# Seven products in place of eight in five of eleven weight blocks of the down projections

## Chip, cores and metric

The kernel runs on one core of a Trainium2 chip. The metric is device time in microseconds (us), the median over runs. One execution was also recorded by the hardware profiler; its durations are used to explain the time.

## What is computed

A trunk of two layers over 256 tokens of width 1024, all in float32. Each layer is a SwiGLU feed-forward (FFN), a mixer (a convolution module in the first layer, latent attention in the second) and another FFN, so there are four FFNs. The part that matters here:

```python
D_MODEL, SEQ, D_FF = 1024, 256, 2816

def swiglu_ffn(h, w1, w3, w2):
    return (jax.nn.silu(h @ w1) * (h @ w3)) @ w2

h = h + 0.5 * swiglu_ffn(rmsnorm(h, g), w1, w3, w2)     # twice in each layer
```

The last product, `@ w2`, is the down projection: (256 x 2816) times (2816 x 1024).

## The kernel before

**Precision.** TensorE is fed with float32r operands. Each float32 operand x is split into `hi`, x rounded to float32r, and `lo = x - hi`. A product of two split operands takes three matmuls into the same accumulator (`mm3`: lo x hi, hi x hi, hi x lo). For weights the split runs on the chip: `load` brings a block of 128 x 2048 float32 (1 MB) into a `raw` buffer by a DMA issued from SyncE (SP), ScalarE casts it to `hi` (two pieces of 1024 columns), and VectorE subtracts to get `lo` (two pieces). There are four `raw` buffers and four pairs of `hi`/`lo` buffers, used in rotation: a raw buffer comes free when its last `lo` is made, a `hi`/`lo` pair when the last matmul that reads it is done.

**One FFN.** In the up part, steps c = 0 to 5 make gate and up columns of the hidden layer. Steps 0 to 4 use four weight blocks each, step 5, half as wide, uses two. For each half of the tokens (tb = 0, 1) the result is multiplied to `g` (VectorE), transposed in 32 x 32 squares (VectorE, `gt`), written to DRAM and read back (`gd`, `gb`, DMAs from SP) and split into `Gh` (ScalarE) and `Gl` (VectorE). This is `turn`. In the down part (`Rows`), eleven weight blocks of `w2` follow, each with two k tiles (128 rows of `w2`) and all 1024 output columns. Four PSUM banks `o[tb, d]` accumulate, one for each half of the tokens and half of the columns. A block is 2 k tiles x 2 token halves x 2 column halves = 8 products of 3 matmuls, 24 matmuls of 512 columns. `block` does blocks 0 to 8; `finish` does blocks 9 and 10 accumulator by accumulator, adds each to the residual `h`, and lets the next stage begin (squares for its norm, transposes `tp` of `h` on TensorE).

**What sets the order.** A scheduler in the build puts the instructions of each engine into one fixed queue. An engine carries out its queue strictly in that order, so an instruction that waits holds up all behind it on the same engine. SP's queue is the order in which DMAs are issued. `urgent` pieces are pulled ahead, and `behind` holds the weight splits back behind them.

Of the kernel before, what the change touches and what calls it, by code (L numbers as in the profile page):

```python
# [41 lines left out]
PIECES = 2  # L42

BEHIND = 6


CONV_DVE = ((0, 0, 31), (2, 0, 31), (4, 0, 31), (5, 0, 31), (7, 0, 13))
# [31 lines left out]
def trunk(ctx: ExitStack, tc: tile.TileContext, x, xt, pos, invf, gains, gfin, wdw,  # L79
# [28 lines left out]
    for i in range(2):  # L108
        for w13, w2 in ((f1w13, f1w2), (f2w13, f2w2)):

            for cc_ in range(5):
                for m in range(2):
                    blocks += [w13[i, m, 2 * cc_ + a_] for a_ in range(2)]
            blocks += [w13[i, a_, 10] for a_ in range(2)]
            blocks += [w2[i, a_] for a_ in range(NF // 2)]
# [24 lines left out]
            order(ins, first)  # L140

    def load(src, pieces=1):
        if isinstance(src, tuple):
            raw = rawp.tile([P, HB], F32, tag="raw", name=uid("raw"))
            nc.sync.dma_start(raw, src[1])
            return raw
        n = src.shape[-1]
        raw = rawp.tile([P, HB], F32, tag="raw", name=uid("raw"))
        hi = wp.tile([P, HB], F32R, tag="hi", name=uid("hi"))
        lo = wp.tile([P, HB], F32R, tag="lo", name=uid("lo"))  # L150
        if len(loaded) < 7:
            fetch(raw[:, :n], src)
        else:
            nc.sync.dma_start(raw[:, :n], src)
        for i in range(pieces):
            c = slice(i * n // pieces, (i + 1) * n // pieces)
            behind(nc.scalar.copy(hi[:, c], raw[:, c]))  # L157
            behind(nc.vector.tensor_sub(lo[:, c], raw[:, c], hi[:, c].bitcast(F32)))  # L158
        return hi, lo

    def urgent(f):

        def g(*args, **kw):
            traced = nc.cur_bb.bb.instructions
            n = len(traced)
            with tc.high_priority():
                r = f(*args, **kw)
            last = {ins.engine: ins for ins in traced[n:]}
            for engine, ins in last.items():
                ahead_of.setdefault(engine, []).append(ins)  # L170
            return r
        return g

    def load_ahead(ahead=W_BUFS - 2):
        load_to(min(len(blocks), n_used[0] + ahead))
# [5 lines left out]
    def weights(n=1, more=True):  # L181
        out = []
        for _ in range(n):
            n_used[0] += 1
            if more:
                load_ahead()
# [279 lines left out]


    class Rows:
        def __init__(self, zh, zl, nk, last=False):
            self.zh, self.zl, self.nk, self.last = zh, zl, nk, last  # L470
            self.o = {(tb, d): bank("A", "o") for tb in range(NT) for d in range(2)}

        def mm(self, part, i, tb, d, o, f0, f1, o0=0, o1=512, after=()):
            hi, lo = part
            for j in range(2):
                f = 2 * i + j
                c = slice(j * D + d * 512 + o0, j * D + d * 512 + o1)
                mm3(o, self.zh[:, f, tbs(tb)], self.zl[:, f, tbs(tb)], hi[:, c], lo[:, c], f == f0, f == f1 - 1,
                    after)

        def block(self, i):
            part, = weights()
            for tb in range(NT):
                for d in range(2):
                    apart = self.last and (tb, d) == (1, 1)
                    self.mm(part, i, tb, d, self.o[tb, d], 0, self.nk - (4 if apart else 0))

        def finish(self, rh, make_next, act):
            nb = self.nk // 2
            parts = weights(2)  # L490

            def add(tb, c, o):
                if rh is None:
                    nc.vector.tensor_add(h[tb][:, c], o, h[tb][:, c])
                else:
                    nc.vector.scalar_tensor_tensor(h[tb][:, c], o, rh[tb], h[tb][:, c],
                                                   op0=ALU.mult, op1=ALU.add)

            if self.last:

# [3 lines left out]
            for i, (tb, d) in enumerate((tb, d) for tb in range(NT) for d in range(2)):  # L504
                halves = self.last and i == 3
                for o0, o1 in ((0, 256), (256, 512)) if halves else ((0, 512),):
                    o, f0 = (bank("B", "o")[:, :256], self.nk - 4) if halves else (self.o[tb, d], 0)
                    for a, part in enumerate(parts):
                        after = nxt.turned if i == 3 and a == 1 and not self.last else ()
                        self.mm(part, nb - 2 + a, tb, d, o, f0, self.nk, o0, o1, after)  # L510
# [15 lines left out]
    def ffn_in(act, X, make_next, beside):  # L526
        Gh = act.tile([P, NF, S], F32R, tag="Gh", name=uid("Gh"))
        Gl = act.tile([P, NF, S], F32R, tag="Gl", name=uid("Gl"))
        def turn(c, tb, w, g):


# [6 lines left out]
                nc.sync.dma_start(dv[i], t[32 * i:32 * i + 32, :w].rearrange("p (j c) -> p j c", j=4))  # L538
            b = act.tile([P, 512], F32, tag="gb", name=uid("gb"), bufs=3)
            nc.sync.dma_start(b[:, :w], d)  # L540
            f = slice(4 * c, 4 * c + n)
            bv = b[:, :w].rearrange("p (i t q) -> p t i q", i=4, q=32)
            gh = Gh[:, f, tbs(tb)].rearrange("p t (i q) -> p t i q", q=32)
            nc.scalar.copy(gh, bv)  # L544
            nc.vector.tensor_sub(Gl[:, f, tbs(tb)].rearrange("p t (i q) -> p t i q", q=32), bv, gh.bitcast(F32))  # L545

        for c in range(6):

# [45 lines left out]
        o = Rows(Gh, Gl, NF, make_next is Final)  # L594
        for i in range(NF // 2 - 2):
            o.block(i)
            beside()
        return o.finish(X.rh, make_next, act)


    def conv(X, make_next):
# [300 lines left out]
    def mla_in(act, X, make_next, cc, sn):  # L902
# [162 lines left out]
        for i in range(2, H + 3):  # L1065
# [5 lines left out]
                values(i - 3, pt[i - 3])  # L1071
            if i in (6, 8):
                o.block((i - 6) // 2)
        return o.finish(None, make_next, act)


    dw = const.tile([P, KT, TAPS], F32, name="dw")
# [121 lines left out]
```

## Time and profile before

| what | value |
|---|---|
| median of 3 runs | 939.93 us (939.67 to 942.21) |
| span of the profiled execution, first to last instruction | 937.9 us |
| granted TensorE clock, mean | 0.997 of full speed |
| TensorE (PE) busy | 925.9 us, 99% of the span |
| VectorE (DVE) busy | 578.2 us, 62% |
| ScalarE (ACT) busy | 493.8 us, 53% |
| GpSimd (POOL) busy | 85.0 us, 9% |
| HBM read and written | 203 GB/s over the span |

The profiled execution's own device time isn't listed apart from its span. The span is 2.0 us below the median of the runs and 1.8 below the fastest; these 2.0 us lie outside the first and last instruction. Matmuls are pipelined: a matmul's listed duration contains time in which the next one already runs, so that a busy share of 99% says that TensorE never waits long, and the pace is read from the starts.

### The profile page before, as it was taken

To read this page: it belongs to the slowest core of one execution; us is meant where nothing else is said; L and a number is where in the kernel's file an instruction comes from. 1 tells how busy PE (TensorE), PEld (TensorE's weight loads), DVE (VectorE), ACT (ScalarE), POOL (GpSimd) and SP (SyncE) were. 2 spreads that over 40 slices of the span, in tenths; PEclk is the share of its full clock that TensorE was granted. 3 is DMA by queue.
4 is the path that set the end of the run, shared out by engine and by line. 5 is a ranking of instruction groups with operands and counts; after the bars stand their busy time and mean duration, and the time that the engine had idled before them with its cause. 6 is when DMAs were issued, how large, how long until landed. Compare 5 with 4: busy or idle time off the path is not lost.

```text
span 937.9 us, 12057 instructions
## 1 busy us (share of the span) xinstructions
PE 925.9 (99%) x4397; PEld 771.7 (82%) x4397; DVE 578.2 (62%) x911; ACT 493.8 (53%) x844; POOL 85.0 (9%) x209
## 2 busy tenths in 40 slices
PE   9999999999999999999999999999999999999997
PEld 6888888898967888888888888888898788888885
DVE  5776664489975655664466666545666576656643
ACT  6964453468865445443374454444666475445431
POOL 1000000059920000000000000000200000000000
PEclk9999999999999999999999999999999999999998
DMA  9986775524324777775547777753441557767611
GB/s 343 355 284 237 245 251 199 179 91 141 130 90 172 277 230 244 245 247 206 197 149 256 239 251 246 236 201 118 180 180 51 189 204 252 244 230 258 233 45 45
DMA packets 60394, 191.54 MB, mean 204 GB/s; under 512 B 11184, under 2 KB 33328, under 8 KB 40752
## 3 DMA queue, kind: packets, MB, share of 16 engines
q1 hardware_dynamic: 59760, 190.09, 58.1%
q8 instruction: 34, 0.56, 0.2%
q10 hardware_dynamic: 576, 0.69, 0.2%
q14 instruction: 24, 0.20, 0.1%
HBM read 178.17 MB, written 12.58 MB: 203 GB/s over the span
## 4 chain that ended last, share of the span: by engine, by line
PE 93%; ACT 3%; DMA 1%; issue 1%; DVE 1%; POOL 1%; SPq 0%; POOLq 0%; ACTq 0%
PE u L240 17%; PE u L244 17%; PE u L243 17%; PE o L240 10%; PE o L243 9%; PE o L244 9%; PE gate L621 3%; PE u L621 3%; PE o L805 2%; ACT hi L157 1%; PE tp L281 1%; DMA raw<-in_f1w 1%; PE a L244 1%; PE a L240 1%; PE a L243 1%
## 5 line engine op out<-in xcount | busy, mean ns | idle before, releaser
L158 DVE TENSOR_TENSOR lo<-raw,hi 128x1024 fp32r<-128x1024 f32 (+1 forms) x290 | 338.9, 1211 | 203.1 <-ACT hi L157 203.0
L157 ACT CAST hi<-raw 128x1024 fp32r<-128x1024 f32 (+1 forms) x290 | 288.1, 1047 | 270.5 <-PE u L244 140.2
L240 PE MATMUL u<-lo,Xh 128*128 128x512 f32 x688 | 268.1, 390 | 0.0
L244 PE MATMUL u<-hi,Xl 128*128 128x512 f32 x688 | 267.7, 390 | 0.4 <-DVE Xl L299 0.4
L243 PE MATMUL u<-hi,Xh 128*128 128x512 f32 x688 | 267.7, 389 | 0.0
L244 PEld LDWEIGHTS u<-hi,Xl 128*128 128x128 f32 x688 | 129.1, 188 | 27.7 <-DVE Xl L299 0.9
L240 PEld LDWEIGHTS u<-lo,Xh 128*128 128x128 f32 x688 | 129.2, 188 | 27.3 <-DVE lo L158 0.5
L243 PEld LDWEIGHTS u<-hi,Xh 128*128 128x128 f32 x688 | 129.2, 188 | 26.5
L243 PE MATMUL o<-hi,Gh 128*128 128x512 f32 (+1 forms) x356 | 137.8, 387 | 0.0
L244 PE MATMUL o<-hi,Gl 128*128 128x512 f32 (+1 forms) x356 | 137.7, 387 | 0.0
L240 PE MATMUL o<-lo,Gh 128*128 128x512 f32 (+1 forms) x356 | 137.3, 387 | 0.0
L244 PEld LDWEIGHTS o<-hi,Gl 128*128 128x128 f32 x356 | 66.9, 188 | 13.6
L243 PEld LDWEIGHTS o<-hi,Gh 128*128 128x128 f32 x356 | 66.9, 188 | 13.4
L240 PEld LDWEIGHTS o<-lo,Gh 128*128 128x128 f32 x356 | 66.8, 188 | 13.4
L272 POOL TENSOR_TENSOR ms<-ss 128x1 f32<-128x1 f32 x16 | 4.6, 287 | 644.5 <-ACT junk L267 644.5
L545 DVE TENSOR_TENSOR Gl<-gb,Gh 128x512 fp32r<-128x512 f32 (+1 forms) x48 | 30.8, 644 | 39.2 <-ACT Gh L544 39.2
L544 ACT CAST Gh<-gb 128x512 fp32r<-128x512 f32 (+1 forms) x48 | 27.9, 584 | 50.8 <-DMA gb<-gd 50.8
L665 DVE SCALAR_TENSOR_TENSOR acc<-V,dw,acc 128x256 f32<-128x256 f32 (+1 forms) x160 | 53.9, 417 | 0.0
L683 ACT ACTIVATE prod<-V,dw 128x128 f32<-128x128 f32 (+1 forms) x121 | 46.1, 421 | 2.9 <-POOL odd L684 1.3
L592 DVE TENSOR_TENSOR g<-s,u 128x512 f32<-128x512 f32 (+1 forms) x48 | 30.7, 639 | 15.9 <-PE u L244 15.5
L590 ACT ACTIVATE s<-u,R 128x512 f32<-128x512 f32 (+1 forms) x48 | 31.2, 650 | 5.9 <-ACT Gh L544 3.0
L534 DVE STREAM_TRANSPOSE gt<-g 128x512 f32<-128x512 f32 (+1 forms) x48 | 32.0, 667 | 1.5
(206 smaller groups left out, 836.1 us busy)
## 6 DMA issues: line engine op xcount, KB each, us to landing
raw<-in_f2w SPq DMA_DIRECT2D x66, 1024.0 KB, 4.9
raw<-in_f1w SPq DMA_DIRECT2D x64, 1024.0 KB, 5.0
raw<-in_cw SPq DMA_DIRECT2D x12, 1024.0 KB, 4.8
gd<-gt SPq DMA_DIRECT2D x160, 64.0 KB, 3.1
gb<-gd SPq DMA_DIRECT2D x40, 256.0 KB, 4.9
raw<-in_wo SPq DMA_DIRECT2D x4, 1024.0 KB, 5.5
raw<-in_wuq SPq DMA_DIRECT2D x3, 1024.0 KB, 4.8
raw<-in_f1w SPq DMA_DIRECT2D x8, 256.0 KB, 6.1
```

Of the source, the lines that this page charges most:

```text
L157: behind(nc.scalar.copy(hi[:, c], raw[:, c]))
L158: behind(nc.vector.tensor_sub(lo[:, c], raw[:, c], hi[:, c].bitcast(F32)))
L240: mm = nc.tensor.matmul(o, ah, bl, start=start, stop=False)
L243: nc.tensor.matmul(o, ah, bh, start=False, stop=False)
L244: return nc.tensor.matmul(o, al, bh, start=False, stop=stop)
L534: nc.vector.transpose(t[:, :w], g[:, :w].rearrange("p (t j q) -> p j t q", t=n, q=32))
L545: nc.vector.tensor_sub(Gl[:, f, tbs(tb)].rearrange("p t (i q) -> p t i q", q=32), bv, gh.bitcast(F32))
L590: nc.scalar.activation(s[:, :w], u[0, tb][:, :w], AF.Silu, scale=X.r[tb])
L592: nc.vector.tensor_mul(g[:, :w], s[:, :w], u[0, tb][:, w:] if both else u[1, tb])
L621: mm = nc.tensor.matmul(u[:, t], w[:, c], X.x[:, k, t], start=(k == 0), stop=(k == KT - 1))
L665: nc.vector.scalar_tensor_tensor(out if j == j1 - 1 else y, v, w, y, op0=ALU.mult, op1=ALU.add)
L683: nc.scalar.activation(p, v, AF.Copy, scale=w)
```

## The change

In blocks 0, 2, 4, 6 and 8 of each down part (the list `FAST`) the eight products become seven by Strassen's scheme in Winograd's form. The 2 x 2 structure is: token halves, the two k tiles of the block, and column halves. It needs sums of the quarters of the weight block (each 128 x 512) and sums of the hidden activations' tiles (128 x 128).

- Weights: a fast block takes two raw buffers and two `hi`/`lo` pairs. Of the raw block three quarters are split (`raw` pair); four sums of quarters are made and split (`sums` pair). GpSimd makes two of the sums in one add of 1024 columns, VectorE the other two in two adds of 512.
- Activations: in the up part, after tb = 1 of steps 0 to 4, GpSimd makes four differences of 128 x 128 (`combine`), which are split by ScalarE and VectorE (`Sh`, `Sl`, and the place in `Gh`, `Gl` of a tile that is no longer needed itself).
- Four of the seven products accumulate over the fast blocks in PSUM banks of their own (`p`: three banks of tag B, one of tag C). After block 8, `fold` adds them to `h` in the right combinations (one copy on ScalarE, four operations on VectorE, four on GpSimd).
- The factor 0.5 / rms, until now applied at the end in `finish`, is applied to `g` in `turn`'s caller.
- `load_ahead` counts slots, so that a fast block counts for two; the SBUF reserve for descriptors of dynamic DMAs is set to 1024.

The core of the diff:

```diff
+FAST = (0, 2, 4, 6, 8)
...
+    def load_fast(src):
+        raw = rawp.tile([P, HB], F32, tag="raw", name=uid("raw"))
+        sums = rawp.tile([P, HB], F32, tag="raw", name=uid("sums"))
+        nc.sync.dma_start(raw, src)
+        v = raw.rearrange("p (b n) -> p b n", n=512)
+        t = sums.rearrange("p (b n) -> p b n", n=512)
+        behind(nc.gpsimd.tensor_tensor(t[:, 0:2, :], v[:, 0:4:3, :], v[:, 1:2, :].to_broadcast([P, 2, 512]), op=ALU.add))
+        behind(nc.vector.tensor_add(t[:, 2, :], t[:, 0, :], v[:, 3, :]))
+        behind(nc.vector.tensor_add(t[:, 3, :], t[:, 2, :], v[:, 2, :]))
+        out = []
+        for x, cols in ((raw, ((0, 512), (1024, 2048))), (sums, ((0, 1024), (1024, 2048)))):
+            hi = wp.tile([P, HB], F32R, tag="hi", name=uid("hi"))
+            lo = wp.tile([P, HB], F32R, tag="lo", name=uid("lo"))
+            for c0, c1 in cols:
+                behind(nc.scalar.copy(hi[:, c0:c1], x[:, c0:c1]))
+                behind(nc.vector.tensor_sub(lo[:, c0:c1], x[:, c0:c1], hi[:, c0:c1].bitcast(F32)))
+            out.append((hi, lo))
+        return out
...
         def block(self, i):
-            part, = weights()
+            part, = weights(1, True, W_BUFS - 1)
...
+        def fast(self, i):
+            n = FAST.index(i)
+            (raw, sums), = weights()
+            if n == 0:
+                self.p = [bank(t, "p") for t in "BBBC"]
...
+            for o, key, (ah, al), (hi, lo), q in (
+                    (self.p[0], "p1", z(f, 0), raw, 0), (self.o[0, 0], (0, 0), z(f + 1, 0), raw, 2),
+                    (self.o[0, 1], (0, 1), s(2), raw, 3), (self.p[2], "p5", z(f, 1), sums, 0),
+                    (self.p[3], "q7", s(1), sums, 1), (self.p[1], "q6", s(0), sums, 2),
+                    (self.o[1, 0], (1, 0), z(f + 1, 1), sums, 3)):
+                c = slice(q * 512, q * 512 + 512)
+                mm3(o, ah, al, hi[:, c], lo[:, c], self.begin(key), isinstance(key, str) and i == FAST[-1])
+            if i == FAST[-1]:
+                self.fold()
...
+        def combine(i, b0, b1):
...
+            sub(v[:, 3], b1[:, 0], b1[:, 1])
+            sub(v[:, 0], b0[:, 0], v[:, 3])
+            sub(v[:, 1], b1[:, 0], b0[:, 0])
+            sub(v[:, 2], b0[:, 1], v[:, 0])
+            split(Sh[:, 3 * n:3 * n + 3, :], Sl[:, 3 * n:3 * n + 3, :], sx[:, :3, :])
+            split(Gh[:, 2 * i, tbs(1)], Gl[:, 2 * i, tbs(1)], sx[:, 3, :])
...
-                nc.vector.tensor_mul(g[:, :w], s[:, :w], u[0, tb][:, w:] if both else u[1, tb])
+                nc.vector.scalar_tensor_tensor(g[:, :w], u[0, tb][:, w:] if both else u[1, tb], X.rh[tb], s[:, :w],
+                                               op0=ALU.mult, op1=ALU.mult)
...
-    nc = _bacc.Bacc("TRN2", target_bir_lowering=False, num_devices=1)
+    nc = _bacc.Bacc("TRN2", target_bir_lowering=False, num_devices=1, dynamic_dma_scratch_size=1024)
```

How the queues change is shown at three places, all in the second FFN (the one behind the convolution; the others read alike). The numbers in the names tell tiles apart. Before, `raw_3650`, `raw_3682`, `raw_3714`, `raw_3746`, `raw_3778` and `raw_3810` are blocks 0 to 5. After, `raw_3697`, `raw_3832`, `raw_3903` and `raw_3974` with `sums_3698`, `sums_3833`, `sums_3904` and `sums_3975` are the fast blocks 0, 2, 4 and 6; `raw_3850` and `raw_3921` are the plain blocks 3 and 5.

**VectorE at the start of the down part.** Before, from `g` of step 5 on:

```order
L592 TENSOR_TENSOR g_3618<-s_3616,u_3566 128x256
L534 STREAM_TRANSPOSE gt_3620<-g_3618 128x256
L545 TENSOR_TENSOR Gl_2714<-gb_3546,Gh_2713 128x4x128
L592 TENSOR_TENSOR g_3633<-s_3631,u_3567 128x256
L534 STREAM_TRANSPOSE gt_3635<-g_3633 128x256
L158 TENSOR_TENSOR lo_3684<-raw_3682,hi_3683 128x1024 x2
L545 TENSOR_TENSOR Gl_2714<-gb_3627,Gh_2713 128x2x128
L158 TENSOR_TENSOR lo_3716<-raw_3714,hi_3715 128x1024 x2
```

After, from the same `g` on:

```order
L687 SCALAR_TENSOR_TENSOR g_3767<-u_3715,rh_2767,s_3765 128x256
L624 STREAM_TRANSPOSE gt_3769<-g_3767 128x256
L604 TENSOR_TENSOR Gl_2814<-gb_3684,Gh_2813 128x3x128
L604 TENSOR_TENSOR Gl_2814<-sx_3686,Gh_2813 128x128
L687 SCALAR_TENSOR_TENSOR g_3782<-u_3716,rh_2848,s_3780 128x256
L181 TENSOR_TENSOR lo_3839<-raw_3832,hi_3838 128x512
L624 STREAM_TRANSPOSE gt_3784<-g_3782 128x256
L181 TENSOR_TENSOR lo_3839<-raw_3832,hi_3838 128x1024
L604 TENSOR_TENSOR Sl_2816<-sx_3686,Sh_2815 128x384
L181 TENSOR_TENSOR lo_3845<-sums_3833,hi_3844 128x1024 x2
L162 TENSOR_TENSOR lo_3852<-raw_3850,hi_3851 128x1024
L173 TENSOR_TENSOR sums_3904<-sums_3904,raw_3903 128x512
```

The subtractions for block 2 stand behind the split of step 4's second token half (`gb_3684`) and behind the difference that GpSimd makes of it (`sx_3686`), as before the split for block 1 stood behind `gb_3546`. The add for block 4 stands between the two halves of block 3's split.

**VectorE in the middle of the down part.** Before, blocks 3 to 5 and on:

```order
L158 TENSOR_TENSOR lo_3748<-raw_3746,hi_3747 128x1024 x2
L158 TENSOR_TENSOR lo_3780<-raw_3778,hi_3779 128x1024 x2
L158 TENSOR_TENSOR lo_3812<-raw_3810,hi_3811 128x1024 x2
L158 TENSOR_TENSOR lo_3844<-raw_3842,hi_3843 128x1024 x2
L158 TENSOR_TENSOR lo_3876<-raw_3874,hi_3875 128x1024 x2
```

After, from block 4 to block 6:

```order
L181 TENSOR_TENSOR lo_3910<-raw_3903,hi_3909 128x512
L181 TENSOR_TENSOR lo_3910<-raw_3903,hi_3909 128x1024
L181 TENSOR_TENSOR lo_3916<-sums_3904,hi_3915 128x1024 x2
L162 TENSOR_TENSOR lo_3923<-raw_3921,hi_3922 128x1024
L173 TENSOR_TENSOR sums_3975<-sums_3975,raw_3974 128x512
L162 TENSOR_TENSOR lo_3923<-raw_3921,hi_3922 128x1024
L174 TENSOR_TENSOR sums_3975<-sums_3975,raw_3974 128x512
L181 TENSOR_TENSOR lo_3981<-raw_3974,hi_3980 128x512
```

The first add for block 6 (`L173`), which needs block 6's data from DRAM and GpSimd's sum of it, stands in front of the second half of block 5's split.

**SP's queue at the start of the down part.** Before:

```order
L538 DMA gd_3541<-gt_3539 32x4x128 x4
L540 DMA gb_3531<-gd_3526 128x512
L154 DMA raw_3746<-in_f2w 128x2048
L540 DMA gb_3546<-gd_3541 128x512
L154 DMA raw_3778<-in_f2w 128x2048
```

After:

```order
L630 DMA gb_3669<-gd_3664 128x512
L628 DMA gd_3679<-gt_3677 32x4x128 x4
L158 DMA raw_3850<-in_f2w 128x2048
L630 DMA gb_3684<-gd_3679 128x512
L169 DMA raw_3903<-in_f2w 128x2048
```

The read-back of step 4's second token half stands behind the DMA of block 3 in both. Block 3's raw buffer is now the one that held block 0's sums.

More of the change, by code (lines that the diff above doesn't have):

```diff
@@ L114, in trunk @@
             blocks += [w13[i, a_, 10] for a_ in range(2)]
-            blocks += [w2[i, a_] for a_ in range(NF // 2)]
+            blocks += [("fast", w2[i, a_]) if a_ in FAST else w2[i, a_] for a_ in range(NF // 2)]
             if w13 is f1w13:
@@ L172, in urgent, with slots @@
         return g
+    def slots(b):
+        return 2 if isinstance(blocks[b], tuple) and blocks[b][0] == "fast" else 1
     def load_ahead(ahead=W_BUFS - 2):
-        load_to(min(len(blocks), n_used[0] + ahead))
+        b = n_used[0]
+        while b < len(blocks) and slots(b) <= ahead:
+            ahead -= slots(b)
+            b += 1
+        load_to(b)
     def load_to(last):
@@ L185, in weights @@
             if more:
-                load_ahead()
+                load_ahead(ahead)
             else:
@@ L468, in trunk, with __init__, begin, mm @@
     class Rows:
-        def __init__(self, zh, zl, nk, last=False):
+        def __init__(self, zh, zl, nk, last=False, sh=None, sl=None):
             self.zh, self.zl, self.nk, self.last = zh, zl, nk, last
+            self.sh, self.sl = sh, sl
             self.o = {(tb, d): bank("A", "o") for tb in range(NT) for d in range(2)}
-        def mm(self, part, i, tb, d, o, f0, f1, o0=0, o1=512, after=()):
+            self.begun = set()
+            self.early = max(i for i in range(nk // 2 - 2) if sh is None or i not in FAST)
+        def begin(self, key):
+            first = key not in self.begun
+            self.begun.add(key)
+            return first
+        def mm(self, part, i, tb, d, o, key, f1, o0=0, o1=512, after=()):
             hi, lo = part
```

70 lines of the change are left out of this document (50 added, 20 removed).

## Prediction

> **What bounds the kernel now.** First the page: busy shares and the chain that ended last.
>
> ```profile
> span 937.9 us, 12057 instructions
> PE 925.9 (99%) x4397; PEld 771.7 (82%) x4397; DVE 578.2 (62%) x911; ACT 493.8 (53%) x844; POOL 85.0 (9%) x209
> PE 93%; ACT 3%; DMA 1%; issue 1%; DVE 1%; POOL 1%; SPq 0%; POOLq 0%; ACTq 0%
> ```
>
> TensorE carries 93% of the chain. Whatever takes a matmul out of an unbroken stream shortens the kernel, as long as the stream stays unbroken. How much one matmul is worth is not its listed duration. The group of down-projection matmuls, then the timeline of TensorE where the second FFN's down part begins:
>
> ```profile
> L240 PE MATMUL o<-lo,Gh 128*128 128x512 f32 (+1 forms) x356 | 137.3, 387 | 0.0
> ```
>
> ```profile
> 411.61 0.39 PE L240 MATMUL o<-lo,Gh 128*128 128x512 f32 x1
> 411.84 0.39 PE L243 MATMUL o<-hi,Gh 128*128 128x512 f32 x1
> ...
> 414.33 0.39 PE L240 MATMUL o<-lo,Gh 128*128 128x512 f32 x1
> ```
>
> The last row is the 12th matmul after the first: 2.72 / 12 = 0.2267 us from start to start. The 387 ns include overlap with the next one. So a block of 24 matmuls lasts 5.44 us, a fast one of 21 lasts 4.76 us.
>
> Next, what the other engines do in the middle of this down part (timeline; the bracket is idle time before):
>
> ```profile
> 433.57 2.01 ACT L157 CAST hi<-raw 128x1024 fp32r<-128x1024 f32 x2 [3.43 <-PE o L244]
> 434.65 2.36 DVE L158 TENSOR_TENSOR lo<-raw,hi 128x1024 fp32r<-128x1024 f32 x2 [3.08 <-ACT hi L157]
> 440.10 2.36 DVE L158 TENSOR_TENSOR lo<-raw,hi 128x1024 fp32r<-128x1024 f32 x2 [3.09 <-ACT hi L157]
> ```
>
> Each block costs VectorE 2.36 of 5.44 us, and the split begins as soon as TensorE releases a buffer pair, three blocks ahead of its use. There is room, and the question is whether the new work fits in it.
>
> **What is removed.** 3 matmuls in each of 5 blocks of 4 FFNs: 60 x 0.2267 = 13.6 us off the stream, 3.4 us for each FFN. (By the listed 387 ns it would be 23.2 us, which is wrong here.) A pair of one fast and one plain block takes TensorE 45 x 0.2267 = 10.20 us, where it took 10.88.
>
> **What is added to a fast block.** The prices, by form:
>
> ```profile
> L158 DVE TENSOR_TENSOR lo<-raw,hi 128x1024 fp32r<-128x1024 f32 x286 | 335.9, 1217 | 203.1 <-ACT hi L157 203.0
> L361 DVE TENSOR_TENSOR lo<-raw,hi 128x512 fp32r<-128x512 f32 x8 | 5.5, 688 | 2.3 <-ACT hi L359 2.2
> L157 ACT CAST hi<-raw 128x1024 fp32r<-128x1024 f32 x286 | 285.4, 1051 | 270.5 <-PE u L244 140.2 <-PE o L244 91.9 <-issue 35.3
> L359 ACT CAST hi<-raw 128x512 fp32r<-128x512 f32 x7 | 4.3, 614 | 3.6 <-DMA raw<-in_f1w 3.6
> L684 POOL TENSOR_TENSOR odd<-odd,prod 128x128 f32<-128x128 f32 x44 | 19.9, 456 | 0.5 <-ACT odd L679 0.5
> L684 POOL TENSOR_TENSOR odd<-odd,prod 128x256 f32<-128x256 f32 x14 | 10.2, 728 | 0.0
> ```
>
> ScalarE: one cast of 512 and three of 1024 columns, 0.61 + 3 x 1.05 = 3.8 us; a pair of blocks 5.9 of 10.2, no bound. VectorE: three subtractions of 1024 (1.18 each in a run, 2.36 / 2), one of 512 and two adds of 512 (0.69 each): 5.6 us; with a plain block 8.0 of 10.2. GpSimd's add of 1024 columns isn't in the trace. The two rows grow by 0.272 us for 128 columns, so an estimate is 0.728 + 6 x 0.272 = 2.36 us. The lower end is VectorE's 1.22 for 1024 columns; the upper end, if the strided and repeated operands cost as much again, is 4.7. I take 2.36, the same engine's own slope.
>
> Separately each engine fits. But VectorE and GpSimd get in each other's way. Timelines of the two in the attention layer, where an add of one column on GpSimd (`ms`) falls beside a subtraction and where it doesn't:
>
> ```profile
> 660.74 3.02 DVE L158 TENSOR_TENSOR lo<-raw,hi 128x640 fp32r<-128x640 f32 x4
> 663.15 0.66 POOL L272 TENSOR_TENSOR ms<-ss 128x1 f32<-128x1 f32 x1 [5.81 <-ACT junk L267]
> 667.01 0.19 POOL L272 TENSOR_TENSOR ms<-ss 128x1 f32<-128x1 f32 x1 [2.01 <-ACT junk L267]
> 669.08 4.62 DVE L158 TENSOR_TENSOR lo<-raw,hi 128x1024 fp32r<-128x1024 f32 x4
> 672.52 1.23 POOL L272 TENSOR_TENSOR ms<-ss 128x1 f32<-128x1 f32 x1 [4.14 <-ACT junk L267]
> ```
>
> Alone the add takes 0.19. Beside a subtraction it takes 0.66 and 1.23 and ends at 663.81 and 673.75, just after VectorE's runs end at 663.76 and 673.70. GpSimd's add waits for the subtraction in progress. That VectorE waits for GpSimd too I take as likely; no row shows it. [...]
>
> Taking turns, a pair of blocks needs 8.0 + 2.4 = 10.4 us of the two engines' time against TensorE's 10.2.
>
> **The chain that decides.** The DMAs and the read-back of `g`:
>
> ```profile
> raw<-in_f2w SPq DMA_DIRECT2D x4, 1024.0 KB, 4.8
> ```
>
> ```profile
> gd<-gt SPq DMA_DIRECT2D x160, 64.0 KB, 3.1
> gb<-gd SPq DMA_DIRECT2D x40, 256.0 KB, 4.9
> ```
>
> Block 6's data needs the raw buffer of block 3, since fast blocks take two of the four. And block 5's second subtraction stands in VectorE's queue behind the first add for block 6. So from "block 3 split" to "block 5 split" there is a chain: DMA 4.8, GpSimd's wait for the subtraction in progress 0 to 1.22 (half, 0.6), its add 2.36, block 5's first half 1.18 (held up by that add), VectorE's add 0.69, the second half 1.18, and some 0.3 of hand-overs (six of 0.05, as 663.81 less 663.76): 11.1 us for each 10.2 of TensorE, 0.9 lost. It is run through for 3 to 5 and 5 to 7.
>
> The first pass, block 1 to block 3, is longer. Time 0 is the end of step 4's products, 48 matmuls before 411.61, or 400.73. Without loss block 3 is due at 10.88 + 4.76 + 5.44 + 4.76 = 25.8. How late the read-back of step 4's second half came before:
>
> ```profile
> 405.81 0.32 SPq L540 DMA_DIRECT2D gb<-gd  x1
> 410.81 0.62 ACT L544 CAST Gh<-gb 128x512 fp32r<-128x512 f32 x1 [1.20 <-DMA gb<-gd]
> ```
>
> It was issued at 5.1 and there at 10.1. Now it is issued behind block 3's DMA, which waits for block 0's sums to be split. VectorE does that behind its `g` (to 1.5) and the wait for GpSimd's add for block 2 (to about 3.0): adds 2 x 0.69, transpose 0.7 and two subtractions 2.4 end at 7.5. The read-back is there at about 13, GpSimd's four differences (4 x 0.456) and the casts end at 16, block 2's raw subtractions (behind them in the queue) at 19.3, GpSimd's add for block 4 at 22.2, then block 2's sums 24.6, block 3's first half 25.8, add and second half 27.7. That is 1.9 late (0 if the read-back isn't held up, 3 if DMAs side by side take 6).
>
> Loss for each FFN: 1.9 + 0.9 + 0.9 = 3.7 us, against 3.4 gained. Four FFNs: +14.8 - 13.6 = +1.2 us. The span becomes 939.1, and with the 2.0 us around it the time is 941.1.
>
> **Edits at nothing.** `g` now multiplies by a third factor, and the last adds have one fewer: the same VectorE form either way. The up part gets 1.8 us of GpSimd (4 x 0.456) and some 0.7 of VectorE (smaller pieces of the same split) in each step of 21.8 us (4 x 5.44), with splits three blocks ahead; if that cover were gone, a step could lose these 2.5. `fold` puts some 3 us on VectorE (4 x 0.75) and four adds of 512 columns, 1.27 each, on GpSimd, before `h` is turned:
>
> ```profile
> 464.13 0.75 DVE L496 SCALAR_TENSOR_TENSOR h<-o,rh,h 128x512 f32<-128x512 f32 x1
> 469.42 0.60 PE L281 MATMUL tp<-ident,h 128*128 128x128 f32 x4
> ```
>
> 4.5 us lie between the add to `h` and its first reader; uncovered it would be up to 3 us for each FFN. The smaller descriptor reserve meets queues that the profile's page lists as made in hardware:
>
> ```profile
> q1 hardware_dynamic: 59760, 190.09, 58.1%
> ```
>
> I price it at nothing; were each DMA slower, the chain above would grow by as much.
>
> **Rivals.** *Slack after all:* GpSimd's add and VectorE's work overlap freely. Then block 5's first half and the wait fall out of the chain: 4.8 + 2.36 + 0.69 + 1.18 + 0.3 = 9.3, under 10.2; block 3 isn't late either, as block 2's sums needn't wait for the add for block 4. Losses of 0.2 for each FFN leave 939.9 - 13.6 + 0.8 = 927.1. For it: GpSimd's waits are the only ones shown. Against it: those two waits. *Slower, GpSimd's add is long:* at its upper end of 4.7 the chain takes 13.4, each pass loses 3.2, the first 1.9 + 2.3: 10.6 for each FFN, 939.9 - 13.6 + 42.4 = 968.7. Each 0.1 over 2.36 costs three passes in four FFNs, 1.2 us, so from 2.5 on the kernel is slower beyond the bound below. For it: nothing in the trace has such operands. Against it: VectorE's price for the same shape is far lower. *Not done:* the products are not fewer, or some matmuls wait for more: 940.
>
> **How the numbers follow.** Changes under 0.3% (2.8 us) are about what a measurement can't tell from none. The forecast, turn-taking with 3.7 lost, has 0.60; its loss lies between 2.0 (half waits, read-back in time) and 5.7 (first pass 3, whole waits), so its own range is 934 to 949, and it splits into faster 0.15, same 0.17, slower 0.28 (with more terms that can grow than shrink). Slack has 0.20 (faster), the long add 0.17 (slower), not done 0.03 (same). Faster 0.35, same 0.20, slower 0.45. The range, 927 to 954, takes in the forecast's own, the first rival's time and the long add up to 3.4 us.
>
> **What would show it.** In the profile after: matmuls still 0.227 apart; idle time of TensorE before blocks 3, 5 and 7 of each down part, put down to `lo`, of 2 and 1 and 1 us; GpSimd's `sums` near 2.4, longer where they meet subtractions; VectorE's subtractions of more than 1.22 beside them; the first add for a fast block waiting for GpSimd. No idle time there would mean slack, and `sums` of over 3 us the long add. Idle time in the up parts or before the transposes would mean that an edit priced at nothing was not.

## The result, and the profile after

The changed kernel took 932.63 us (median of 4, 930.08 to 935.65), the kernel before beside it 939.80: a ratio of 0.9923, interval 0.9896 to 0.995. It is faster; the forecast was 941.1 and leaned to slower. Two of the four times lie at 930 and two at 935. The profiled execution is the one of 930.08 us: 9.6 us of span were gained there of the 13.6 that left the stream, and some 5 fewer in the other two.

The page of after, the lines that answer to those of before:

```profile
span 928.3 us, 12409 instructions
PE 913.5 (98%) x4337; PEld 761.0 (82%) x4337; DVE 687.6 (74%) x1047; ACT 536.4 (58%) x928; POOL 213.4 (23%) x325
PE 89%; DVE 5%; ACT 3%; DMA 1%; issue 1%; SPq 0%; POOLq 0%; ACTq 0%; POOL 0%; DVEq 0%
```

There are 60 matmuls fewer, VectorE's share went from 62% to 74%, GpSimd's from 9% to 23%, and VectorE is now on 5% of the chain where it was on 1%. TensorE's timeline in the second FFN's down part, at the first matmuls of blocks 0, 2 and 7:

```profile
411.13 0.39 PE L271 MATMUL p<-lo,Gh 128*128 128x512 f32 x1
...
421.33 0.39 PE L271 MATMUL p<-lo,Gh 128*128 128x512 f32 x1
...
446.49 0.39 PE L271 MATMUL o<-lo,Gh 128*128 128x512 f32 x1
```

A pair of a fast and a plain block takes 10.20 us, exactly 45 x 0.2267, and blocks 0 to 6 (three pairs and a fast block) 35.36 = 30.60 + 4.76. The stream is unbroken. What TensorE did wait for is in the view of waits (in all, times, longest):

```profile
PE tp L433 <- ACT sigm L422: 2.9, 1, 2.9
PE o L271 <- ACT Oh L1151: 1.3, 2, 0.9
PE o L901 <- ACT Z L837: 1.1, 1, 1.1
```

The first row is new, and no row says `lo` before a down block. So the losses of 1.9, 0.9 and 0.9 us that the prediction put into every FFN aren't there. Where the 4.0 us went, by the times at which TensorE's stages begin:

| stretch | before | after | off the stream | lost |
|---|---|---|---|---|
| to the first down part | 127.06 | 127.24 | 0 | 0.2 |
| first down part, to the transposes of the conv's norm | 58.49 | 58.11 | 3.4 | 3.0 |
| from there to the second down part | 226.06 | 225.78 | 0 | -0.3 |
| to the third down part | 181.41 | 178.52 | 3.4 | 0.5 |
| to the fourth (attention in between) | 277.88 | 275.23 | 3.4 | 0.75 |
| to the end | 67.00 | 63.42 | 3.4 | -0.2 |

Three quarters lie in one place, the end of the first FFN. VectorE's and GpSimd's timelines there:

```profile
169.33 4.60 DVE L162 TENSOR_TENSOR lo<-raw,hi 128x1024 fp32r<-128x1024 f32 x3 [1.59 <-ACT hi L161]
173.85 0.68 DVE L553 TENSOR_TENSOR fold<-p,fold 128x512 f32<-128x512 f32 x1
174.45 1.21 DVE L162 TENSOR_TENSOR lo<-raw,hi 128x1024 fp32r<-128x1024 f32 x1
175.58 0.68 DVE L554 TENSOR_TENSOR fold<-p,fold 128x512 f32<-128x512 f32 x1
176.19 0.67 DVE L556 TENSOR_TENSOR fold<-p,fold 128x512 f32<-128x512 f32 x1
176.78 4.18 DVE L162 TENSOR_TENSOR lo<-raw,hi 128x1024 fp32r<-128x1024 f32 x2
180.88 0.68 DVE L558 TENSOR_TENSOR fold<-p,fold 128x512 f32<-128x512 f32 x1
181.48 1.87 DVE L566 TENSOR_TENSOR h<-o,h 128x512 f32<-128x512 f32 x3
```

```profile
177.60 2.28 POOL L557 TENSOR_TENSOR h<-h,fold 128x512 f32<-128x512 f32 x1
```

VectorE does not pause from 169.33 until the additions to `h` (`L566`) are done. The split of the last down block, `fold`, and the split of two blocks of the next stage stand ahead of them, and one pair of subtractions takes 4.18 in place of 2.36 us because GpSimd's addition of 2.28 lies in it. The second `h` addition starts at 182.1. Before, the same queue held only one split:

```profile
177.31 2.36 DVE L158 TENSOR_TENSOR lo<-raw,hi 128x1024 fp32r<-128x1024 f32 x2 [3.08 <-ACT hi L157]
179.58 0.74 DVE L496 SCALAR_TENSOR_TENSOR h<-o,rh,h 128x512 f32<-128x512 f32 x1
181.66 0.75 DVE L496 SCALAR_TENSOR_TENSOR h<-o,rh,h 128x512 f32<-128x512 f32 x1 [1.33 <-PE o L244]
184.41 0.29 DVE L396 TENSOR_SCALAR dR<-ident,R 128x128 f32<-128x128 f32 x1 [2.00 <-POOL R L275]
```

There the `h` additions waited for TensorE, and the norm's factor (`dR`) was ready at 184.70, 0.85 us before its transposes at 185.55. With 3.4 us off the stream the second addition should have started at about 178.4; it came 3.7 later, less 0.85 of cover: the wait of 2.9. (The row of the wait names `sigm`, a small step that ScalarE does behind the same squares. It ended at 185.24; `dR`, which the transposes read, ended at 185.25.)

### The profile page after: what moved, and what is told of

It is laid out like the page before. It is cut to its first block, busy times and chain, and to the rows that moved or that the text cites. A ratio compares the mean times of both kernels' runs of the same rounds, so it can differ in the third digit from the quotient of the medians.

```text
span 928.3 us, 12409 instructions
## 1 busy us (share of the span) xinstructions
PE 913.5 (98%) x4337; PEld 761.0 (82%) x4337; DVE 687.6 (74%) x1047; ACT 536.4 (58%) x928; POOL 213.4 (23%) x325
## 4 chain that ended last, share of the span: by engine, by line
PE 89%; DVE 5%; ACT 3%; DMA 1%; issue 1%; SPq 0%; POOLq 0%; ACTq 0%; POOL 0%; DVEq 0%
PE u L275 17%; PE u L271 17%; PE u L274 17%; PE o L271 6%; PE o L274 6%; PE o L275 6%; DVE lo L162 3%; PE u L717 3%; PE gate L717 3%; PE p L275 2%; PE p L271 2%; PE p L274 2%; PE o L901 2%; PE y L790 2%; ACT hi L161 1%
## 5 line engine op out<-in xcount | busy, mean ns | idle before, releaser
L162 DVE TENSOR_TENSOR lo<-raw,hi 128x1024 fp32r<-128x1024 f32 (+1 forms) x250 | 304.9, 1255 | 76.9 <-ACT hi L161 76.8
L161 ACT CAST hi<-raw 128x1024 fp32r<-128x1024 f32 (+1 forms) x250 | 248.0, 1046 | 153.3 <-PE u L275 111.1
L271 PE MATMUL o<-lo,Gh 128*128 128x512 f32 (+1 forms) x236 | 91.0, 386 | 0.0
L275 PE MATMUL o<-hi,Gl 128*128 128x512 f32 (+1 forms) x236 | 91.0, 385 | 0.0
L274 PE MATMUL o<-hi,Gh 128*128 128x512 f32 (+1 forms) x236 | 91.0, 385 | 0.0
L172 POOL TENSOR_TENSOR sums<-raw 128x1024 f32<-128x1024 f32 x20 | 53.1, 2653 | 161.2 <-DMA raw<-in_f2w 52.6
L181 DVE TENSOR_TENSOR lo<-sums,hi 128x1024 fp32r<-128x1024 f32 x40 | 56.1, 1433 | 0.0
L180 ACT CAST hi<-sums 128x1024 fp32r<-128x1024 f32 x40 | 40.7, 1052 | 22.5 <-PE u L275 15.3
L604 DVE TENSOR_TENSOR Gl<-gb,Gh 128x512 fp32r<-128x512 f32 (+2 forms) x48 | 33.1, 704 | 26.4 <-ACT Gh L603 26.4
L180 ACT CAST hi<-raw 128x512 fp32r<-128x512 f32 (+1 forms) x40 | 31.4, 834 | 34.7 <-PE o L275 27.8
```

The lines of the kernel that those rows point to most:

```text
L172: behind(nc.gpsimd.tensor_tensor(t[:, 0:2, :], v[:, 0:4:3, :], v[:, 1:2, :].to_broadcast([P, 2, 512]), op=ALU.add))
L180: behind(nc.scalar.copy(hi[:, c0:c1], x[:, c0:c1]))
L181: behind(nc.vector.tensor_sub(lo[:, c0:c1], x[:, c0:c1], hi[:, c0:c1].bitcast(F32)))
L271: mm = nc.tensor.matmul(o, ah, bl, start=start, stop=False)
L274: nc.tensor.matmul(o, ah, bh, start=False, stop=False)
L275: return nc.tensor.matmul(o, al, bh, start=False, stop=stop)
```

## Experiments

Theory A, from that trace: the weights of the down blocks are ready in time, and what is lost lies at the ends of the FFNs, in VectorE's queue. Rival B: VectorE and GpSimd taking turns in the down blocks costs it. Rival C: the prediction's chain.

**The changed kernel again,** twice, for a profile of the longer time and for its spread. Theory D in the second expectation is A with what the first run added; it is spelled out under hold_subs.

> The changed kernel once more, unaltered, beside the others of this call. Its four times stood at two levels, 930.1 and 930.7, and 934.6 and 935.7, and only the lower one has a trace. Theory A (the weights of the down blocks are ready in time; what was not gained, 4.0 of 13.6 us in that trace, lies where an FFN ends: about 3 us where the h additions of the first FFN come behind fold and the next blocks' differences, some 0.5 us each behind the second and third) says nothing of the upper level: a profile at that level should show it in some other place. Rival B (VectorE and GpSimd taking turns in the down blocks): at the upper level TensorE waits for lo or sums in the down blocks, some 5 us in all. Rival C (the prediction's chain, 0.9 us for each pass and 1.9 us for the first): waits of 0.9 us before plain blocks 3, 5 and 7. Expected times: 930 to 936.

> The changed kernel unaltered, beside the next three. Theory D says its time depends on how late the weights of the first FFN run: 930 to 931 where its first down block is fetched by 105 us after the start of the span, 933 to 936 where it is fetched some 2.6 us later.

Measured: 934.50 (933.18 to 936.27, 5 runs) and 931.51 (929.74 to 934.54, 6 runs); ratios 0.9947 (0.9935 to 0.9959) and 0.9915 (0.9903 to 0.9928). With the first four that is a spread from 929.7 to 936.3, not two levels. The profile of `again`, at 934.50: the waits, ScalarE and VectorE where the last down block is split, TensorE at the transposes, and the window from 188 to 190 us (the figure after the five engines is the granted clock):

```profile
PE tp L433 <- ACT sigm L422: 4.8, 1, 4.8
```

```profile
171.22 2.00 ACT L161 CAST hi<-raw 128x1024 fp32r<-128x1024 f32 x2 [5.35 <-DMA raw<-in_f1w]
```

```profile
172.30 2.36 DVE L162 TENSOR_TENSOR lo<-raw,hi 128x1024 fp32r<-128x1024 f32 x2 [2.00 <-ACT hi L161]
```

```profile
188.32 3.45 PE L433 MATMUL tp<-dR,h 128*128 128x128 f32 x16 [4.84 <-ACT sigm L422]
```

```profile
188.00:190.00 2.00, 1.68 (x8) 1.71 (x9) 0.22 (x1) 0.82 (x4) 0.00 (x0) 0.50 0.02 8
```

It is the same place, worse. The last down block's cast came 3 us later (171.22, in after 168.24), now waiting for its data: the DMA was issued 2.6 us later and took 7.1 us to land, in place of 4.9. Why it took longer isn't shown. The whole queue moved, and TensorE waited 4.84 us. Behind this wait its clock is 0.50: the 16 transposes take 3.45 us, in after 2.02. From the conv's second transposes on the two traces run alike. The sum of 4.4 us: 0.98 at the first down part's start, 2.0 more of wait, 1.4 of slow clock. The longer time goes with how late the first FFN's weights run. Four traces of the changed kernel show it (`late`, told below, has one transfer more); the second and third column give when the DMA of block 1 was issued and when that of block 10 had landed:

| trace | block 1 issued | block 10 landed | block 10 split from | wait | clock behind it | time |
|---|---|---|---|---|---|---|
| after | 104.93 | 166.42 | 169.33 | 2.87 | 1.00 | 930.08 |
| again2 | 105.59 | 167.15 | 169.32 | 2.87 | 1.00 | 930.10 |
| late | 106.64 | 169.80 | 170.98 | 4.19 | 0.50 | 934.56 |
| again | 107.52 | 171.12 | 172.30 | 4.84 | 0.50 | 934.50 |

What makes the weights late in one run and not in another is open.

So the expectation of `again` that the upper time has another place was wrong, and rivals B and C, which wanted waits in the down blocks, don't find them in this trace.

**The next stage's blocks held back.** First with casts and differences, at the first FFN's end only:

```diff
-            parts = weights(2)
+            parts = weights(2, n_used[0] > 40)
...
-                        nxt.early(i)
+                        nxt.early(i); i == 0 and load_ahead()
```

> At the end of the first FFN the next two blocks are loaded and split behind the first h addition and not ahead of all of them, so that VectorE goes from fold straight to the h additions. The other FFNs are as they were. Theory A: the wait of 2.9 us ahead of the transposes of the conv's norm goes to under 0.5 us, and the time is 2.4 to 2.9 us below that of the changed kernel (about 927.5 against 930.4, and the same step at the upper level). Rivals B and C: the loss is in the down blocks, and the time stays within 0.5 us.

Measured: 933.99 (932.51 to 934.34), ratio 0.9938 (0.9926 to 0.9949); beside `again` no gain where 2.4 to 2.9 us were expected. The wait was 3.45. ScalarE's timeline tells why:

```profile
179.99 0.63 ACT L298 ACTIVATE junk<-h 128x512 f32<-128x512 f32 x1 [6.04 <-DVE h L566]
180.52 0.19 ACT L298 ACTIVATION_READ_ACCUMULATOR junk<-h 128x1 f32 x1
180.62 3.88 ACT L161 CAST hi<-raw 128x1024 fp32r<-128x1024 f32 x4
184.40 0.63 ACT L298 ACTIVATE junk<-h 128x512 f32<-128x512 f32 x1
```

VectorE's `h` additions now came on time (179.20 and 180.63, each waiting for TensorE), but the held casts went in between the two squares on ScalarE. The wait changed engines, so this run decides nothing. The second form leaves the casts where they were and holds the differences alone:

```diff
...
-            behind(nc.vector.tensor_sub(lo[:, c], raw[:, c], hi[:, c].bitcast(F32)))
+            rest = lambda c=c: behind(nc.vector.tensor_sub(lo[:, c], raw[:, c], hi[:, c].bitcast(F32)))
+            held.append(rest) if holding[0] else rest()
...
+            holding[0] = n_used[0] < 40
             parts = weights(2)
+            holding[0] = False
...
                         nxt.early(i)
+                    while i == 1 and held:
+                        held.pop(0)()
```

> At the end of the first FFN only the differences (lo) of the next two blocks are put behind the second h addition; their casts on ScalarE stay early, so that neither VectorE nor ScalarE has anything of the next stage ahead of the h additions and squares. Theory D: at the upper level the transfers of the first FFN run some 2.6 us late, the last down block is split late, fold, the four differences and the h additions queue up on VectorE, TensorE waits over 3 us for the transposes, and its clock halves for 3 us behind that; at the lower level only the wait of 2.9 us is there. Without the four differences in that queue the wait falls under 1 us and the clock stays: 927.5 to 929.5, against 930.4 and 934.5 of the changed kernel. Rival E: late transfers alone make the upper level, through waits in front of the last down blocks: then these waits stay and the time stays above 932.

Measured: 928.38 (927.61 to 928.64), ratio 0.9879 (0.9862 to 0.9895). The waits have no row for `tp` any more. VectorE's timeline:

```profile
174.02 0.69 DVE L554 TENSOR_TENSOR fold<-p,fold 128x512 f32<-128x512 f32 x1
...
175.95 0.68 DVE L559 TENSOR_TENSOR fold<-p,fold 128x512 f32<-128x512 f32 x1
177.59 0.69 DVE L569 TENSOR_TENSOR h<-o,h 128x512 f32<-128x512 f32 x1 [0.96 <-PE o L276]
179.02 0.69 DVE L569 TENSOR_TENSOR h<-o,h 128x512 f32<-128x512 f32 x1 [0.74 <-PE o L276]
181.79 0.29 DVE L428 TENSOR_SCALAR dR<-ident,R 128x128 f32<-128x128 f32 x1 [2.08 <-POOL R L307]
```

This profile's weights ran late as well: block 10 landed at 170.56, and block 6 began 10.50 us and block 8 10.92 us after the block two before, in place of 10.20. Even so the additions waited for TensorE, nothing was lost at the transposes, and the four times lie within 1.0 us, where the 15 of the changed kernel spread over 6.5. This is the theory's test by removal, and it holds; rival E's 932 is ruled out. The changed kernel was not run beside hold_subs, so that the two are compared by their ratios to the kernel before; beside `late_hold_dve` below it was (`again2`).

The held differences are not free. They now stand ahead of the first part of the next stage's input (`Xp`) in VectorE's queue, and TensorE waits there:

```profile
PE gate L722 <- DVE Xp L445: 0.7, 1, 0.7
```

From the transposes to the second down part this trace takes 226.61 us, 0.8 more than after.

**Four fast blocks in place of five.**

```diff
-FAST = (0, 2, 4, 6, 8)
+FAST = (0, 2, 4, 6)
```

> Blocks 0, 2, 4 and 6 in seven products; block 8 is plain, so that fold comes 10.9 us earlier in each FFN, with four plain blocks behind it. The stream saves 48 matmuls in place of 60, 10.9 in place of 13.6 us. Theory A and D: nothing of fold stands ahead of the h additions any more, the losses at the ends of the FFNs (0.5 to 4.4 us each) are gone, and the time is 939.6 less 10.9, 928.7 to 930: no slower than the changed kernel at its lower level and some 4 us faster than at its upper one. If the loss isn't at the ends of the FFNs, each fast block is worth the same: 2.7 us above the changed kernel, 933 to 937.

Measured: 929.28 (928.75 to 930.17), ratio 0.9891 (0.9876 to 0.9906): 10.3 of the 10.9 us that it takes off the stream, against 7.2 of 13.6 (939.80 less 932.63) of the changed kernel. Its second FFN with what follows it lasts 178.70 us, 181.41 less 12 x 0.2267 to 0.01; in after 0.5 were lost there. Its first FFN had the latest weights of all these traces (block 1 issued at 108.28), and yet no wait for `tp`. Beside the profiled runs of 930, the fifth fast block with `fold` at its end is worth nothing as the change places it.

**The products without the gain.** The product for p5 is issued twice in each fast block.

```diff
+                if key == "p5":
+                    mm3(o, ah, al, hi[:, c], lo[:, c], self.begin(key), False)
```

> The fast blocks issue the product for p5 twice, so that a fast block has 24 matmuls as a plain one has; the preparation, the read-back, GpSimd's work and fold are all there. p5 is then counted twice, so the output is not the reference's. It parts the gain of the stream from the price of everything else. Theory A: 60 matmuls at 0.2267 us are 13.6 us more than the changed kernel, some 944, 4 us above the kernel before: that is the price of the ends of the FFNs. Rivals B and C: the waits in the down blocks shrink by what the blocks are longer, so it is 9 to 11 us above the changed kernel, 940 to 941, and one level is left of the two.

Measured: 944.12 (943.59 to 947.75), ratio 1.0059 (1.0046 to 1.0072). With as long a stream as before, everything else that the scheme adds costs 4.5 us. In the profile nothing waits for `lo` in the down blocks. The wait for `tp` is 1.1, and behind the second and third FFN TensorE waits 1.1 us each for `Xl`, the `lo` part of the next stage's input. The profiled run stands 14.0 us above that of after, as theory A had it; beside `again`, run on the same chip, it is 9.6, which fits a longer stream that covers part of the late queue. The spread didn't go.

**The chain of the weights, lengthened and shortened.** GpSimd's addition (`L172`) issued twice; and the same addition once, on VectorE:

```diff
+        behind(nc.gpsimd.tensor_tensor(t[:, 0:2, :], v[:, 0:4:3, :], v[:, 1:2, :].to_broadcast([P, 2, 512]), op=ALU.add))
```

> GpSimd's addition of 1024 columns is issued twice with the same result, so that it takes 4.8 in place of 2.4 us in the chain from one fast block's transfer to the next. In the second FFN's trace the plain blocks 3, 5 and 7 were ready 2.4, 2.0 and 1.1 us before their turn and a pass took 10.53 us for 10.20 us of TensorE. Theory D: a pass takes 12.9 us; block 3 is just in time, blocks 5 and 7 wait some 2.5 us each: 5 to 6 us for each FFN, 952 to 957 in all. The prediction's chain without slack: 2.4 us in each of 12 places, 29 us, 961 to 965. If the chain has far more slack than that trace shows: within 2 us of the changed kernel.

```diff
-        behind(nc.gpsimd.tensor_tensor(t[:, 0:2, :], v[:, 0:4:3, :], v[:, 1:2, :].to_broadcast([P, 2, 512]), op=ALU.add))
+        behind(nc.vector.tensor_tensor(t[:, 0:2, :], v[:, 0:4:3, :], v[:, 1:2, :].to_broadcast([P, 2, 512]), op=ALU.add))
```

> The addition of 1024 columns in load_fast goes from GpSimd to VectorE, so that GpSimd has no part in the weights and the two engines do not take turns there. VectorE has 1.2 us more for each fast block, 9.2 of 10.2 us for a pair. Theory A: the weights were in time before, so the time stays within 0.7 us of the changed kernel. Rival B: what the taking of turns costs comes back, 3 to 5 us, above all the upper level. Rival C: the chain of a pass loses the 2.4 us addition and gains 1.2, so it is under 10.2 us: 2 to 4 us come back.

Measured for the doubled one: 953.43 (952.53 to 953.81), ratio 1.0146 (1.0131 to 1.0161). Its waits:

```profile
PE o L272 <- DVE lo L162: 9.5, 7, 2.2
PE tp L434 <- ACT sigm L423: 4.2, 1, 4.2
PE p L272 <- DVE lo L182: 2.9, 2, 1.4
```

The prediction's waits appear, where a pass is 2.4 us longer. The second, third and fourth FFN lose 5.1, 5.6 and 5.0 us against after, within theory D's 5 to 6, though mostly in one pass: in the second FFN block 5 was still in time and blocks 6 and 7 together took 14.77 in place of 10.20. Without slack it would have been 29 us in all. Measured for the addition on VectorE: 931.54 (930.03 to 933.08), ratio 0.9915 (0.9902 to 0.9927). Its profile, at 930.03, has the stretches of after within 0.05 us: 58.14 in the first FFN's down part (after 58.11), 178.54, 275.19 and 63.43 from the second, third and fourth on (178.52, 275.23, 63.42). A pass shorter by 1.7 us gains nothing there. Beside `again`, run on the same chip, it is 3.0 us less, which theory A didn't expect and rival C did. A shorter pass that catches up on late weights would do that, but in this trace the weights were not late (block 1 issued at 103.51). The two intervals don't overlap, but with `again2` at 931.51 on another occasion I don't call it shown.

**Both remedies.** hold_subs with the addition on VectorE.

> hold_subs and the addition of 1024 columns on VectorE together. A pass of the down chain is then 8.9 us (one transfer of a fast block to the next was 8.86 us with the addition on VectorE, 10.53 us with it on GpSimd) and catches up on late transfers by 1.3 us a pass. Theory D: 927 to 928.5 with a spread under 2 us. Rival E: as add_on_dve alone, about 930 to 932.5.

Measured: 928.28 (927.88 to 928.92), ratio 0.988 (0.9865 to 0.9895): as theory D has it, and in time no better than hold_subs alone. In its trace the first down part, up to the transposes, loses nothing (55.1 us, 58.49 less 3.4), where that of hold_subs lasts 56.12.

**Late weights made on purpose.** A transfer of half an MB that nothing uses, in the first FFN's up part, in three kernels:

```diff
-            nc.sync.dma_start(raw[:, :n], src)
+            at = nc.sync.dma_start(raw[:, :n], src)
+        if len(loaded) == 14:
+            spare = dram.tile([P, 1024], F32, name="spare")
+            order(nc.sync.dma_start(spare, f1w2[0, 0][:, :1024]), at.ins)
```

> The changed kernel with a half MB transfer from memory to memory put behind a weight block in the middle of the first FFN's up part (its result is used by nothing), which takes some 3 us of the transfers there. Theory D: the weights of the first FFN are then late in every run, so the lower level is gone: all times 933 to 938, with a wait over 3 us ahead of the transposes of the conv's norm and TensorE at half clock behind it. If the upper level has another cause, the time stays at 930 to 936 as without it.

> The kernel before with the same transfer of half an MB. It parts what the late transfers cost by themselves from what they cost with the fast blocks. Theory D: the down part of the kernel before has 10.88 us for a pair of blocks and nothing of fold ahead of its h additions, so it takes them up: within 0.7 us of the kernel before. Otherwise 2 to 4 us slower, as the changed kernel.

> hold_subs_dve with the same transfer of half an MB. Theory D: with the differences of the next blocks behind the h additions and a pass of 8.9 us in the down chain, the late weights are taken up: 928 to 929.5, within 1 us of hold_subs_dve. Otherwise 931 to 934.

Measured: 932.27 (930.63 to 934.56), 939.36 (939.11 to 940.35), ratio 1.0 (0.9991 to 1.0008), and 927.83 (927.67 to 927.86), ratio 0.9875 (0.9861 to 0.989). The first is a miss: beside again2 it is only 0.8 us more, within the spread. The transfer made block 1's fetch later by 1 us (106.64 against 105.59), not by 3, and the lower times did not go. That the transfer is what made the profiled run late is therefore not shown. This run, at 934.56, has the same chain of events once more:

```profile
187.00 3.75 PE L436 MATMUL tp<-dR,h 128*128 128x128 f32 x16 [4.19 <-ACT sigm L425]
```

```profile
188.00:190.00 2.00, 2.00 (x11) 2.00 (x11) 0.00 (x0) 0.00 (x0) 0.00 (x0) 0.50 0.00 0
```

The kernel before takes the transfer up without a trace, but as it did little to the changed kernel either, that says little about late weights. The kernel with both remedies has the smallest time of all, 11.7 us under the kernel before, and its four times lie within 0.2 us, where those of the changed kernel beside it (again2) spread over 4.8. What remains between it and 939.5 less 13.6 is 1.9 us.

## Why the prediction was wrong, step by step

**Right.** The stream: 13.6 us by 0.2267 for a matmul, not 23 by the listed 387 ns; pairs last 10.20. GpSimd's addition: estimated 2.36, and the rows of after (shortest, median and longest in ns):

```profile
L172 POOL TENSOR_TENSOR sums<-raw x20: 2392/2401/3874, 98.6 to 892.5; 128x1024 f32<-128x1024 f32 x20
```

```profile
L181 DVE TENSOR_TENSOR lo<-sums,hi x40: 1180/1217/3440, 119.4 to 901.3; 128x1024 fp32r<-128x1024 f32 x40
```

The two engines do take turns in this trace, and in both directions: GpSimd's 2.40 becomes up to 3.87 (at 607.06), VectorE's 1.22 up to 3.44 (at 416.30, beside GpSimd's addition that ends at 418.66). The kernel before had shown GpSimd's waits alone; that VectorE waits too I had assumed, and no row of before shows it. So *Slack after all* came nearest with its 927.1, but its reason, free overlap, is false. A pass of the chain came near too: 11.1 predicted, and from block 5's split to block 7's in the second FFN it is 11.14 (434.28 to 445.42). That it agrees so closely is luck: GpSimd's addition began 0.16 us after the data had landed, without the 0.6 of waiting in the sum, and the second add for block 8 (0.69), which the sum leaves out, stood ahead of block 7's second half. From 3 to 5 it is 10.53, as there block 5's first half had begun (428.95) before GpSimd's addition (429.70) and was not held up.

**Wrong: "That is 1.9 late", the first pass.** VectorE and GpSimd in the second FFN, time 0 of the prediction being 400.25:

```profile
414.71 1.21 DVE L181 TENSOR_TENSOR lo<-raw,hi 128x1024 fp32r<-128x1024 f32 x1
...
416.30 4.58 DVE L181 TENSOR_TENSOR lo<-sums,hi 128x1024 fp32r<-128x1024 f32 x2
420.80 1.21 DVE L162 TENSOR_TENSOR lo<-raw,hi 128x1024 fp32r<-128x1024 f32 x1
421.94 0.68 DVE L173 TENSOR_TENSOR sums<-sums,raw 128x512 f32<-128x512 f32 x1
422.54 1.21 DVE L162 TENSOR_TENSOR lo<-raw,hi 128x1024 fp32r<-128x1024 f32 x1
```

```profile
416.00 2.66 POOL L172 TENSOR_TENSOR sums<-raw 128x1024 f32<-128x1024 f32 x1 [1.24 <-DVE lo L181]
```

Block 2's raw subtractions ended at 15.7, not 19.3; GpSimd's addition for block 4 at 18.4, not 22.2; block 3 was split at 23.5, not 27.7, and due at 25.8. It came 2.3 us early, where 1.9 late was predicted. Two terms were too long. The read-back was there at 11.4, not 13: VectorE's wait for GpSimd's sum for block 2 ended at 1.7, not 3.0, so that block 0's sums were split at 5.9, not 7.5. And I put the raw subtractions behind the four differences and all casts, where the order that I quoted has them between: they need only a cast, and VectorE began them at 13.5, while GpSimd was still subtracting (to 14.5).

**Wrong as a consequence: "Loss for each FFN: 1.9 + 0.9 + 0.9".** A pass that is longer than TensorE's costs nothing while the block comes early. The passes took 0.3 and 0.9 of the 2.3 us, and block 7 was still 1.1 us in time. After that there is no further pass. So of the 14.8 us predicted for four FFNs none stands in the down blocks of after, and most of the 4.0 us lost there lies where the prediction had priced `fold` at nothing. `add_twice` shows the same chain from the other side: 2.4 us more for each pass, and the waits are there. And where the lead was used up, in the first FFN of the profiles of hold_first (10.49, 10.51 and 10.96 us for its last three pairs) and hold_subs (10.50 and 10.92), the passes cost what they take beyond 10.20: 0.3 and 0.7 to 0.8, the term's mechanism at its true size.

**Wrong: "Edits at nothing", `fold`.** The cover named was 4.5 us between an `h` addition and its first reader, from the second FFN. The first FFN ends in another norm: its transposes need the factor of the whole row, and there the cover was 0.85 us. I also counted only fold's own 3 us, not what stands beside it in VectorE's queue: the next stage's four differences, 4.8 us, and turn-taking with fold's own additions on GpSimd (1.8 in the row of 4.18, 1.1 in that of 4.60). That the sentence "up to 3 us for each FFN" uncovered fits the 3.0 of the first FFN in after is luck, since `fold` was only a part of that queue; the others lost 0.5 and 0.75, the last none. What no term foresaw is that TensorE's granted clock was 0.50 behind this wait in `again` and `late`, and that the wait goes with how late the transfers run (2.87 to 4.84 us in the table above).

**The 0.5 and 0.75 us behind the second and third FFN.** The trace of after places most of them. Behind the second:

```profile
467.58 1.47 PE L312 MATMUL tp<-ident,h 128*128 128x128 f32 x12
...
469.79 0.51 PE L275 MATMUL u<-hi,Xl 128*128 128x512 f32 x1 [0.28 <-DVE Xl L330]
```

TensorE has twelve transposes in a row, directly ahead of the next stage's first matmuls, and then waits for `Xl`, which is made from what they return. Before, and in `four`, three groups of four stand among the last block's matmuls, and this wait is not there. It costs 0.44 us from start to start, and as much once more behind the third FFN (648.30). VectorE was idle for 0.85 us ahead of `Xl`, which points to the place of the transposes in TensorE's queue and not to VectorE's queue; no run tested it. The other 0.3 us behind the third FFN are not placed, and whether `fold` at the end or the fifth fast block as such moved the transposes was not parted.

## What to carry to other kernels

A chain that is longer than the loop it feeds costs nothing until its lead is used up: work out the lead at the first pass and the number of passes, and only what goes beyond is lost. What a change adds at the end of a stage is to be priced at each stage's own next reader, with all that already stands in the same queue, since covers differ (0.85 and 4.5 us here). And moving work out of one engine's queue can put it into another's: look at every engine that has a part of the moved step.

## What was not expected of the hardware

Ahead of the transposes, TensorE's granted clock fell to 0.54 at a wait of 3.45 (`hold_first`, over the window from 188 to 190 us) and to 0.50 at waits of 4.16 (`add_twice`), 4.19 (`late`) and 4.84 us (`again`), and stayed at 1.00 at waits of 1.1 (`eight`), 2.87 (after, `again2`) and 2.9 (`add_on_dve`). It was back some 3 to 6 us after matmuls began again, at a price of 1.4 to 2.8 us in `again`, `hold_first` and `late` (mean granted clock over the span 0.996, 0.996 and 0.995, in after 0.998). But the length of the wait alone doesn't decide in these runs. In the first FFN's down part of `add_twice` the clock was at 0.50 behind a wait of 2.17 us, shorter than one that left it at 1.00 (the row behind the wait, and the window from 156 to 157 us):

```profile
155.35 0.80 PE L272 MATMUL o<-lo,Gh 128*128 128x512 f32 x1 [2.17 <-DVE lo L162]
```

```profile
156.00:157.00 1.00, 1.00 (x4) 0.81 (x3) 1.00 (x2) 0.34 (x1) 0.00 (x0) 0.50 0.83 147
```

GpSimd's addition with strided and repeated operands took 2.40 us alone (`L172` of after, the median of 20), close to the 2.36 estimated from the two rows on plain ones.
